# Dense products and attention scores as single float32 products in a two-layer hybrid diffusion trunk step

## The chip, the cores and the metric

The kernel runs on one core of one Trainium2 chip. The metric is the device time of one execution, in microseconds (us). TensorE does the matrix products, VectorE (DVE), ScalarE (ACT) and GpSimd (POOL) the rest, SyncE (SP) issues most loads. All tensors in DRAM are float32.

## What is computed

Two layers over 640 tokens (512 latent, 128 context) of 1024 channels. Each layer has an attention half with four parallel mixers and a feed-forward half with a width-3 convolution; both halves are normed before and after and modulated by a conditioning vector.

```python
def sandwich_layer(x, cvec, mixers, lp):
    mod = jax.nn.silu(cvec) @ lp['w_mod'] + lp['b_mod']
    sh1, sc1, g1, sh2, sc2, g2 = jnp.split(mod, 6, -1)
    h = rmsnorm(x, lp['g_attn_pre']) * (1 + sc1) + sh1
    pa, pb, pc, pd = jnp.split(h @ lp['w_in'], [IN_A, IN_A + IN_B, IN_A + IN_B + IN_C], -1)
    branches, ctx_state = mixers(pa, pb, pc, pd)
    br = jnp.stack(branches, 2)
    gates = jax.nn.sigmoid(h @ lp['w_gate'] + lp['b_gate']).reshape(h.shape[0], h.shape[1], N_BRANCH, D_MODEL)
    merged = jnp.sum(gates * jnp.einsum('blkc,kcd->blkd', br, lp['w_branch']), 2)
    x = x + g1 * rmsnorm(merged @ lp['w_out'], lp['g_attn_post'])
    h = rmsnorm(x, lp['g_ffn_pre']) * (1 + sc2) + sh2
    x = x + g2 * rmsnorm(conv_ffn(h, lp['ffn_w_up'], lp['ffn_conv'], lp['ffn_w_down']), lp['g_ffn_post'])
    return x, ctx_state

def conv_ffn(h, w_up, conv_w, w_down):
    L = h.shape[1]
    u = h @ w_up
    pad = CONV_W // 2
    up = jnp.pad(u, ((0, 0), (pad, CONV_W - 1 - pad), (0, 0)))
    uc = up[:, 0:L] * conv_w[0]
    for j in range(1, CONV_W):
        uc = uc + up[:, j:j + L] * conv_w[j]
    a, gt = jnp.split(uc, 2, -1)
    return (jax.nn.silu(gt) * a) @ w_down
```

The mixers are a 2-D neighbourhood attention (A), a latent attention with low-rank keys (B), a windowed attention with a sink (C) and a pooling mixer (D); A, B and C have four heads each. Latent tokens also read the context keys.

## The kernel before

Operands of the dense products and of the scores are split into two float32r tensors, a high and a low part. `load` brings a weight unit of 128 x 1024 into a `raw` tile (two buffers), and `split` makes the parts: a copy to float32r on ScalarE (L144) and a subtraction on VectorE (L145). The activations that are multiplied with weights are split in the same way when they are written. A dense product is then three products that add up in one PSUM bank:

```python
nc.tensor.matmul(ps, lhsT=hi[:, k, :], rhs=self.hT[:, 0, k, o:o + n], start=k == 0, stop=False)
nc.tensor.matmul(ps, lhsT=hi[:, k, :], rhs=self.hT[:, 1, k, o:o + n], start=False, stop=False)
nc.tensor.matmul(ps, lhsT=lo[:, k, :], rhs=self.hT[:, 0, k, o:o + n], start=False, stop=k == KT - 1)
```

These are lines 536 to 538 (`tposed`: weights stationary, 640 tokens moving in chunks of 384 and 256 columns; the projections of A and D, the gates, and the feed-forward's up projection). Lines 515 to 517 (`nat_step`) have the tokens stationary and 256, 352 or 512 weight columns moving, lines 548 to 550 (`sweep`) the same with 512 for the output and down projections, and lines 1227 to 1229 the branches' products in `gates`. The scores (line 946, `products`) are two such products for A and C and three for B. What multiplies probabilities by values (L938), turns tiles (L155), makes the latent attention's keys, values and queries (L1116, L1122, L1140) and the modulation rows (L370) is plain float32 already.

A layer first runs `attention_phase`. There the order of TensorE's instructions is that in which the code issues them, and `weave` makes it: a chain, such as the attention steps of `pipeline`, yields a time wherever its next product has to wait for other engines, and pieces of a fill (projections or a branch's gates) are issued until the times that they yield in turn add up to it:

```python
for want in chain:
    want -= over
    while want > 0:
        took = next(fill, None)
        if took is None:
            break
        want -= took
    over = max(0, -want)
```

An attention step turns the probabilities of the step before, makes its scores (in two rounds for A and B), and then multiplies the turned probabilities with the values. It asks for the times in `FILL`, 1400 for each pause in the transposes, and a lead at the start. The chain of C is filled with the projections of D and A; those of B's projection, of A and of B with the gates of D, C and A. The gates of B come last, since they need B's output. `out_phase` and `ffn_phase` follow. The feed-forward's 22 hidden tiles go in five groups (`GRP`): `up_pair` makes a group's tiles, `down` projects the group before and adds its part to the sum in `acc`. Layer 1's three modulation banks (`mod_bank`, 8 steps of 4 products each) stand between the hidden tiles of layer 0; those of layer 0 in its attention phase.

Of the kernel before, what the change touches and what calls it, by code (L numbers as in the profile page):

```python
# [12 lines left out]
F32R = mybir.dt.float32r  # L13
# [17 lines left out]
GRP = (4, 4, 4, 4, 6)  # L31
# [16 lines left out]
C_N = C_INV + 2  # L48

# [47 lines left out]
class Kernel:  # L97
# [22 lines left out]
    # ---------------------------------------------------------------- weights  # L120
    def load(self, src, a, b):
        raw = self.t(self.rawp, [128, 1024], "raw", bufs=2)
        rv = raw[:, :a * b].rearrange("p (a b) -> p a b", b=b)
        for j, x in enumerate(src if isinstance(src, list) else [src]):
            p = x.shape[0]
            self.nc.sync.dma_start(out=rv[p * j:p * j + p], in_=x)
        return raw, a, b

    def parts(self, loaded):
        """Loaded weights as two float32r parts."""  # L130
        raw, a, b = loaded
        n = a * b
        w = self.t(self.wp, [128, 2, 1024], "w", F32R)
        self.split(w[:, 0, :n], w[:, 1, :n], raw[:, :n])
        v = w[:, :, :n].rearrange("p s (a b) -> p s a b", b=b)
        return v[:, 0], v[:, 1]

    def unit(self, src, a, b):
        return self.parts(self.load(src, a, b))

    def split(self, hi, lo, src, scale=None):
        nc = self.nc
        if scale is None:
            nc.scalar.copy(hi, src)  # L144
            nc.vector.tensor_tensor(out=lo, in0=src, in1=hi.bitcast(F32), op=ALU.subtract)  # L145
        else:
            nc.scalar.mul(hi, src, scale)
            nc.vector.scalar_tensor_tensor(out=lo, in0=src, scalar=scale, in1=hi.bitcast(F32),
                                           op0=ALU.mult, op1=ALU.subtract)
# [7 lines left out]
    # ---------------------------------------------------------------- set up  # L157
    def run(self):
        nc, tc = self.nc, self.tc
        from contextlib import ExitStack  # L160
        with ExitStack() as es:
            es.enter_context(nc.allow_low_precision("operands split exactly into two float32r parts"))
# [3 lines left out]
            self.wp = es.enter_context(self.pool("w", bufs=5))  # L166
            self.rawp = es.enter_context(self.pool("raw", bufs=2))
# [9 lines left out]
            self.hT = self.t(self.hp, [128, 2, KT, TOK], "hT", F32R)  # L177
# [9 lines left out]
            mod = [self.mod_bank(0, b, hold) for b in (1, 2)]  # L187
            for l in range(self.depth):
                self.attention_phase(l, mod if l == 0 else None, banks if l == 0 else None)
                self.ffn_phase(l)  # L190

    def start(self):
        """Layer 0's first modulation, its normed input and its first projection, by blocks of channels: each
        block's columns of the modulation weights are loaded, its channels modulated, and its products summed."""
# [5 lines left out]
        with self.pool("start", bufs=8) as sp:  # L200
# [5 lines left out]
            for t in range(NT):  # L206
                junk = self.t(self.hp, [128, 2, 1280], "yx", bufs=2)[:, 0, :D]
                self.normed(x[:, t, :], x[:, t, :], junk)
# [41 lines left out]
    def start_products(self, banks, block, unit):  # L250
        hi, lo = unit
        for a in range(block[1]):
            for t in range(NT):
                self.nat_step(banks[t], t, block[0] + a, hi[:, a, :], lo[:, a, :])

    def modulate_block(self, ks, x):
        """Channel tiles ks of all token tiles: transpose, modulate and split into hT."""
        nc = self.nc
        mc = self.lay[0]['mc']
        f = self.t(self.hp, [128, 2, 1280], "yx", bufs=2)[:, 0, :].rearrange("p (k n) -> p k n", k=2)  # L260
        last = self.t(self.psp, [128, 512], "tr", bufs=PSB["tr"])
        for j, kk in enumerate(range(ks.start, ks.stop)):
# [5 lines left out]
            for s, o, n, src in ((0, 0, 512, ps), (1, 512, 128, last[:, 128 * j:128 * j + 128])):  # L268
                a, b = mc[:, 0, 0, s, kk:kk + 1], mc[:, 0, 1, s, kk:kk + 1]
                if j == 0:  # L270
                    nc.scalar.activation(f[:, j, o:o + n], src, AF.Identity, scale=a, bias=b)
                else:
                    nc.vector.tensor_scalar(f[:, j, o:o + n], src, a, b, op0=ALU.mult, op1=ALU.add)
            self.split(self.hT[:, 0, kk, :], self.hT[:, 1, kk, :], f[:, j, :])

    def cond(self):
        nc = self.nc
        raw = self.t(self.rawp, [128, 1024], "raw", bufs=2)[:16]
# [53 lines left out]
    def small(self, l):  # L332
        """The convolution's taps: loads, and a step later their transposes."""
# [20 lines left out]
    # -------------------------------------------------------- modulation rows  # L354
    def mod_bank(self, l, b, hold, late=0):
        """Rows 2b and 2b + 1 of the modulation, by 128 rows of its weights: each load a step ahead of the products."""
        nc, i = self.nc, self.i

        def load(k):
            w = self.t(self.wp, [128, 2048], "w")  # L360
            nc.sync.dma_start(out=w, in_=i['w_mod'][l, 128 * k:128 * k + 128, b * 2048:b * 2048 + 2048])
            return w
# [4 lines left out]
        for k in range(KT):  # L367
            ahead = load(k + 1) if k + 1 < KT else None
            for g in range(4):
                nc.tensor.matmul(ps[32 * g:32 * g + 2, :], lhsT=self.sc[:, k, :], rhs=w[:, 512 * g:512 * g + 512],  # L370
# [23 lines left out]
    def with_steps(self, gen, steps):  # L394
        """gen's pieces with one of steps after each."""
# [5 lines left out]
    def mod_rows(self, l, b, ps, rows):  # L401
        """Modulation rows 2b and 2b+1 of both streams; gates go to DRAM."""
# [1294 lines left out]
```

## Time and profile before

| | |
|---|---|
| median of three runs | 2185.11 us (2182.93 to 2186.3) |
| the profiled execution: its span, which is the time that the profile gives of it | 2180.6 us |
| TensorE busy | 2130.0 us (98% of the span), 13815 products |
| VectorE busy | 1216.8 us (56%) |
| ScalarE busy | 855.7 us (39%) |
| GpSimd busy | 183.3 us (8%) |
| DMA | 221.74 MB, mean 102 GB/s |

The span runs from the first to the last instruction of the program. A product's record is longer than its share of TensorE's time, as products are pipelined; how fast they follow each other is seen from the starts in the timeline. All products are called f32 in the profile, float32r ones too.

### The profile page before, as it was taken

What the parts mean: (1) busy time and instruction counts of PE and PEld (TensorE: products, weight loads), DVE (VectorE), ACT (ScalarE), POOL (GpSimd) and SP (SyncE); (2) the same over time, 40 slices, a digit from 0 to 9 for tenths busy, and PEclk for the clock granted to TensorE, in tenths of its full rate; (3) what the DMA queues carried; (4) which work ended last, traced back from release to release, by engine and by line L of the source; (5) the groups of instructions that cost most, each with busy time, mean ns of one, the idle gap of its engine ahead of it and who ended that gap; (6) DMA issues with size and microseconds to landing.
All of it is one profiled execution on the core that took longest, in us unless ns stands there. A gap on an engine that the chain in (4) does not pass through costs nothing.

```text
span 2180.6 us, 34629 instructions
## 1 busy us (share of the span) xinstructions
PE 2130.0 (98%) x13815; PEld 1928.2 (88%) x13815; DVE 1216.8 (56%) x2207; ACT 855.7 (39%) x1822; POOL 183.3 (8%) x574
## 2 busy tenths in 40 slices
PE   7999999999999999999999999999999999999998
PEld 4779989998889988989878799999998899999996
DVE  3774454653466636456577744556543665556554
ACT  4554344443353333224255543434433533323322
POOL 1102100001021001000021031000000200000001
PEclk9999999999999999999999999999999999999999
DMA  9513221214544444343332132211124322222222
GB/s 303 202 43 101 56 62 46 59 40 156 186 144 150 152 136 156 116 155 89 120 128 81 38 92 64 59 48 52 38 79 154 117 78 78 78 78 78 78 85 94
DMA packets 230476, 221.74 MB, mean 102 GB/s; under 512 B 16084, under 2 KB 196637, under 8 KB 225195
## 3 DMA queue, kind: packets, MB, share of 16 engines
q1 hardware_dynamic: 214000, 191.91, 28.3%
q10 hardware_dynamic: 12026, 21.55, 2.8%
q0 software_dynamic: 4288, 6.07, 1.1%
q8 instruction: 109, 1.79, 0.3%
q14 instruction: 53, 0.43, 0.1%
HBM read 207.94 MB, written 11.56 MB: 101 GB/s over the span
## 4 chain that ended last, share of the span: by engine, by line
PE 89%; DVE 4%; issue 2%; ACT 2%; DMA 1%; POOL 1%; ACTq 0%; DVEq 0%; POOLq 0%
PE mm L536 17%; PE mm L538 16%; PE mm L537 16%; PE mm L548 5%; PE mm L550 5%; PE mm L549 5%; PE tr L155 4%; PE sc L946 3%; PE py L938 2%; PE mm L1227 2%; PE mm L1229 2%; PE mm L1228 2%; PE py L370 1%; PE sc L548 1%; PE sc L549 1%
## 5 line engine op out<-in xcount | busy, mean ns | idle before, releaser
L536 PE MATMUL mm<-hT,w 128*128 128x384 f32 (+1 forms) x2592 | 821.6, 317 | 1.2 <-ACT slab L859 0.9
L538 PE MATMUL mm<-hT,w 128*128 128x384 f32 (+1 forms) x2592 | 801.6, 309 | 1.5 <-DVE w L145 1.5
L537 PE MATMUL mm<-hT,w 128*128 128x384 f32 (+1 forms) x2592 | 800.7, 309 | 0.0
L536 PEld LDWEIGHTS mm<-hT,w 128*128 128x128 f32 x2592 | 491.0, 189 | 33.4 <-issue 17.1
L538 PEld LDWEIGHTS mm<-hT,w 128*128 128x128 f32 x2592 | 491.0, 189 | 3.1 <-DVE w L145 3.1
L537 PEld LDWEIGHTS mm<-hT,w 128*128 128x128 f32 x2592 | 491.4, 190 | 2.0 <-issue 1.4
L145 DVE TENSOR_TENSOR w<-raw,w 128x1024 fp32r<-128x1024 f32 (+2 forms) x263 | 313.4, 1194 | 133.0 <-ACT w L144 131.5
L144 ACT CAST w<-raw 128x1024 fp32r<-128x1024 f32 (+2 forms) x263 | 269.3, 1027 | 205.0 <-PE mm L550 37.3
L1364 DVE TENSOR_SCALAR cv<-ub,taps 128x641 f32<-128x641 f32 x86 | 47.7, 555 | 203.3 <-ACT ub L1358 192.9
L1366 DVE SCALAR_TENSOR_TENSOR cv<-ub,taps,cv 128x641 f32<-128x641 f32 x172 | 152.2, 885 | 5.4
L548 PE MATMUL mm<-w,gT 128*128 128x512 f32 (+1 forms) x352 | 141.4, 402 | 0.0
L549 PE MATMUL mm<-w,gT 128*128 128x512 f32 (+1 forms) x352 | 138.9, 394 | 0.0
L550 PE MATMUL mm<-w,gT 128*128 128x512 f32 (+1 forms) x352 | 138.8, 394 | 0.0
L1209 ACT ACTIVATE th<-mm,cols 128x384 f32<-128x384 f32 (+1 forms) x128 | 67.4, 527 | 148.2 <-PE mm L538 147.9
L1355 ACT COPY ub<-mm 128x384 f32<-128x384 f32 x86 | 41.4, 481 | 164.5 <-PE mm L538 164.4
L1236 DVE SCALAR_TENSOR_TENSOR th<-th,mm 128x384 f32<-128x384 f32 x96 | 45.8, 483 | 100.6 <-PE mm L1229 92.7
L548 PEld LDWEIGHTS mm<-w,gT 128*128 128x128 f32 (+1 forms) x352 | 66.2, 188 | 23.8 <-issue 7.4
L1357 ACT COPY ub<-mm 128x128 f32<-128x128 f32 x86 | 23.0, 267 | 162.4 <-PE mm L538 162.3
L1227 PE MATMUL mm<-yx,w 128*128 128x384 f32 (+1 forms) x256 | 82.8, 323 | 0.0
L1429 DVE TENSOR_TENSOR acc<-acc,mm 128x512 f32<-128x512 f32 x64 | 44.0, 687 | 65.3 <-PE mm L550 64.7
L155 PE MATMUL tr<-cst,P 128*128 128x128 f32 x462 | 67.1, 275 | 13.2 <-DVE P L914 9.2
L550 PEld LDWEIGHTS mm<-w,gT 128*128 128x128 f32 (+1 forms) x352 | 66.0, 188 | 15.7
(305 smaller groups left out, 3152.1 us busy)
## 6 DMA issues: line engine op xcount, KB each, us to landing
w<-in_w_mod_dram SPq DMA_DIRECT2D x46, 1024.0 KB, 4.8
raw<-in_ffn_w_up_dram SPq DMA_DIRECT2D x84, 512.0 KB, 3.9
raw<-in_w_gate_dram SPq DMA_DIRECT2D x64, 512.0 KB, 4.0
raw<-in_ffn_w_down_dram SPq DMA_DIRECT2D x40, 512.0 KB, 3.7
raw<-in_w_in_dram SPq DMA_DIRECT2D x23, 512.0 KB, 4.1
raw<-in_w_out_dram SPq DMA_DIRECT2D x16, 512.0 KB, 6.7
x<-x ACTq DMA_DIRECT2D x14, 512.0 KB, 4.8
raw<-in_w_branch_dram SPq DMA_DIRECT2D x12, 512.0 KB, 3.2
```

What stands on the lines that cost most here:

```text
L144: nc.scalar.copy(hi, src)
L145: nc.vector.tensor_tensor(out=lo, in0=src, in1=hi.bitcast(F32), op=ALU.subtract)
L155: self.nc.tensor.transpose(out, in_, ident)
L536: nc.tensor.matmul(ps, lhsT=hi[:, k, :], rhs=self.hT[:, 0, k, o:o + n], start=k == 0, stop=False)
L537: nc.tensor.matmul(ps, lhsT=hi[:, k, :], rhs=self.hT[:, 1, k, o:o + n], start=False, stop=False)
L538: nc.tensor.matmul(ps, lhsT=lo[:, k, :], rhs=self.hT[:, 0, k, o:o + n], start=False, stop=k == KT - 1)
L548: nc.tensor.matmul(ps, lhsT=lh[:, c], rhs=hi, start=q == 0, stop=False)
L549: nc.tensor.matmul(ps, lhsT=lh[:, c], rhs=lo, start=False, stop=False)
L550: nc.tensor.matmul(ps, lhsT=ll[:, c], rhs=hi, start=False, stop=q == n - 1)
L1209: self.anchor = nc.scalar.activation(th[:, :n], pg[:, :n], AF.Tanh, scale=0.5, bias=L['bh'][:, 8 * br + m:8 * br + m + 1]).ins
L1227: nc.tensor.matmul(pb[:, :n], lhsT=hi[:, 0, ms], rhs=y[:, 0, a, cs], start=a == 0, stop=False)
L1366: nc.vector.scalar_tensor_tensor(out=cv, in0=ub[:, j:j + 641], scalar=tp[:, j:j + 1], in1=cv, op0=ALU.mult, op1=ALU.add)
```

## The change

Weights stay as they are loaded: `unit` loads straight into one of 16 tiles of 128 x 1024 (pool `w`), and `load`, `parts`, `split`, `split_queries`, `split_keys` and the class `Latent` go. Activations are written once, in float32. Each dense product is one float32 product, and so is each product of the scores. The times that pieces of fill yield are worked out anew, from `PER`. The feed-forward keeps all 22 hidden tiles (`gT`, 22 buffers) and has one down projection. Of layer 1's modulation banks the second and third move from the feed-forward of layer 0 into layer 1's attention phase. The factors of one half that went with the splits of `merged` and of the hidden tiles go too; the norm behind each takes `4 * EPS` instead.

```diff
-GRP = (4, 4, 4, 4, 6)
+WBUFS = 16
+PER = 0.842
...
+def took(n):
+
+    return PER * n
...
     def tposed(self, ps, w, c, k0=0, k1=KT):
         o, n = c
         for k in range(k0, k1):
-            nc.tensor.matmul(ps, lhsT=hi[:, k, :], rhs=self.hT[:, 0, k, o:o + n], start=k == 0, stop=False)
-            nc.tensor.matmul(ps, lhsT=hi[:, k, :], rhs=self.hT[:, 1, k, o:o + n], start=False, stop=False)
-            nc.tensor.matmul(ps, lhsT=lo[:, k, :], rhs=self.hT[:, 0, k, o:o + n], start=False, stop=k == KT - 1)
+            self.nc.tensor.matmul(ps, lhsT=w[:, k, :], rhs=self.hT[:, k, o:o + n], start=k == 0, stop=k == KT - 1)
...
         def step(ps, q, o):
-            lh, ll, hi, lo = parts[q]
-            c = slice(o, o + 128)
-            nc.tensor.matmul(ps, lhsT=lh[:, c], rhs=hi, start=q == 0, stop=False)
-            nc.tensor.matmul(ps, lhsT=lh[:, c], rhs=lo, start=False, stop=False)
-            nc.tensor.matmul(ps, lhsT=ll[:, c], rhs=hi, start=False, stop=q == n - 1)
+            lhs, w = parts[q]
+            self.nc.tensor.matmul(ps, lhsT=lhs[:, o:o + 128], rhs=w, start=q == 0, stop=q == n - 1)
...
-    def products(self, outs, parts):
-        """outs[j] = the sum of the products of the pairs in parts[j]."""
-        n = len(parts[0])
-        for q in range(n):
-            for out, p in zip(outs, parts):
-                self.nc.tensor.matmul(out, lhsT=p[q][0], rhs=p[q][1], start=q == 0, stop=q == n - 1)
+    def pair(self, outs, parts):
+
+        for out, (lhs, rhs) in zip(outs, parts):
+            self.nc.tensor.matmul(out, lhsT=lhs, rhs=rhs, start=True, stop=True)
...
             r, ct = self.HALF[j], slice(128 * t, 128 * t + 128)
-            return (x[:, j, a, ct], kk[:, j, c]), (ql[r, a, ct], kk[r, j, c])
+            return x[r, a, ct], kk[r, c]
...
     def between(self, gen, mod):
         for took in gen:
             yield took
             if next(mod, None):
-                yield 850
+                yield 430
...
                     self.tposed(pg[:, :n], u, (o, n), k0, k1)
-                    yield 3 * (k1 - k0) * (n / 2.4 + 2.5)
+                    yield (k1 - k0) * took(n)
...
                 for a in range(2):
-                    hi, lo = wb[a]
-                    nc.tensor.matmul(pb[:, :n], lhsT=hi[:, 0, ms], rhs=y[:, 0, a, cs], start=a == 0, stop=False)
-                    nc.tensor.matmul(pb[:, :n], lhsT=hi[:, 0, ms], rhs=y[:, 1, a, cs], start=False, stop=False)
-                    nc.tensor.matmul(pb[:, :n], lhsT=lo[:, 0, ms], rhs=y[:, 0, a, cs], start=False, stop=a == 1)
-                yield 6 * (n / 2.4 + 2.5)
+                    nc.tensor.matmul(pb[:, :n], lhsT=wb[a][:, 0, ms], rhs=y[:, a, cs], start=a == 0, stop=a == 1)
+                yield 2 * took(n)
...
+            for k in range(2, 22):
+                gts += self.up_pair(l, [k])
+                next(mod, None)
+            self.drain(mod)
+            self.down(l, gts)
```

`FILL`, `PROJ_C_FILL`, `A_LEAD` and the 1400 of the transposes stay. In the changed kernel line 505 is the product of `tposed`, 492 of `nat_step`, 513 of `sweep`, 1155 of the branches, 879 of the scores, 873 of probabilities and values, 140 the transposes.

The change moves instructions on TensorE. The first place is the latent attention of layer 0, in the middle of its steps. Before, a step reads so (`tr` are the banks of the transposes, `P` the probabilities, `sc` the scores, `mm_4803` a gate's bank, `py` the output):

```order
L155 MATMUL tr_4757<-cst_75,P_4677 128x128 x4
L155 MATMUL tr_4763<-cst_75,P_4714 128x128 x4
...
L946 MATMUL sc_4783<-slab_3797,stg_4723 128x320 x2
L946 MATMUL sc_4783<-slab_3797,stg_4724 128x320
...
L536 MATMUL mm_4803<-hT_79,w_4688 128x384
L537 MATMUL mm_4803<-hT_79,w_4688 128x384
L538 MATMUL mm_4803<-hT_79,w_4688 128x384
...
L946 MATMUL sc_4822<-slab_3797,stg_4723 128x320 x2
L946 MATMUL sc_4822<-slab_3797,stg_4724 128x320
...
L938 MATMUL py_4848<-pt_4756,v_3528 64x128 x10
```

And in the changed kernel, from the last gate product before B's own gates on:

```order
L1155 MATMUL mm_3049<-yx_2004,w_2386 128x256
L1155 MATMUL mm_3049<-yx_2004,w_2433 128x256
L879 MATMUL sc_3054<-ka_2453,qa_2452 128x320
L879 MATMUL sc_3055<-ka_2453,qa_2452 128x320
L873 MATMUL py_2985<-pt_3007,v_2454 64x128 x10
L140 MATMUL tr_3083<-cst_72,P_3039 128x128 x4
L140 MATMUL tr_3089<-cst_72,P_3063 128x128 x4
L140 MATMUL tr_3095<-cst_72,P_3039 128x128
L140 MATMUL tr_3095<-cst_72,P_3063 128x128
L879 MATMUL sc_3100<-ka_2453,qa_2452 128x320
L879 MATMUL sc_3101<-ka_2453,qa_2452 128x320
L879 MATMUL sc_3112<-ka_2453,qa_2452 128x320
```

The gate products that stood between a step's scores have gone ahead of it; what follows, up to B's gates, are transposes, scores and products of the attention alone: five whole steps, the second half of another, and two of the context. Layer 1 has the same.

The second place is the end of the window attention. In the changed kernel (`cb` and `acc` hold keys and queries; the last row is the next projection) it reads:

```order
L873 MATMUL py_856<-pt_1011,T_447 64x128 x6
L140 MATMUL tr_1059<-cst_72,P_1034 128x128 x4
L879 MATMUL sc_1068<-cb_446,acc_445 128x384
...
L140 MATMUL tr_1097<-cst_72,P_1070 128x128 x3
...
L879 MATMUL sc_1109<-cb_446,acc_445 128x512
L879 MATMUL sc_1110<-cb_446,acc_445 128x512
...
L140 MATMUL tr_1141<-cst_72,P_1111 128x128 x4
...
L492 MATMUL mm_1270<-w_1275,hT_76 128x352 x2
```

Before, products of lines 536 to 538 stood between those scores and transposes; now the last four steps follow each other without any, in both layers.

## Rows read from the trace of the kernel before

**Rows 1.** The page: busy time of each engine, and the chain by engine.

```profile
PE 2130.0 (98%) x13815; PEld 1928.2 (88%) x13815; DVE 1216.8 (56%) x2207; ACT 855.7 (39%) x1822; POOL 183.3 (8%) x574
...
PE 89%; DVE 4%; issue 2%; ACT 2%; DMA 1%; POOL 1%; ACTq 0%; DVEq 0%; POOLq 0%
```

**Rows 2.** TensorE's largest group by line and form: count | busy us, mean ns.

```profile
L536 PE MATMUL mm<-hT,w 128*128 128x384 f32 x1296 | 444.3, 343 | 0.4 <-ACT hT L144 0.4
```

**Rows 3.** TensorE's timeline, three places: start us, duration us, engine, line, tiles.

```profile
502.70 0.33 PE L536 MATMUL mm<-hT,w 128*128 128x384 f32 x1
...
503.22 0.33 PE L536 MATMUL mm<-hT,w 128*128 128x384 f32 x1
...
505.98 0.28 PE L536 MATMUL mm<-hT,w 128*128 128x256 f32 x1
...
506.34 0.28 PE L536 MATMUL mm<-hT,w 128*128 128x256 f32 x1
...
1121.63 0.39 PE L548 MATMUL mm<-w,gT 128*128 128x512 f32 x1
...
1122.10 0.40 PE L550 MATMUL mm<-w,gT 128*128 128x512 f32 x1
```

**Rows 4.** Line 1116's records, and the timeline around plain float32 products.

```profile
L1116 PE MATMUL sc<-cb x24: 377/378/381, 341.4 to 1427.6; 128*128 128x256 f32 x24
...
344.40 1.03 PE L1116 MATMUL sc<-cb 128*128 128x256 f32 x4
...
345.38 0.28 PE L537 MATMUL mm<-hT,w 128*128 128x256 f32 x1
...
347.92 1.02 PE L1122 MATMUL sc<-cb 128*128 128x512 f32 x2
...
348.95 0.34 PE L1228 MATMUL mm<-yx,w 128*128 128x384 f32 x1
```

**Rows 5.** The timeline of all engines over one step of the latent attention.

```profile
412.76 1.03 PE L155 MATMUL tr<-cst,P 128*128 128x128 f32 x8
...
413.45 0.59 ACT L924 COPY pt<-tr 128x512 f32<-128x512 f32 x1 [0.84 <-PE tr L155]
...
415.36 1.13 PE L946 MATMUL sc<-slab,stg 96*128 96x320 f32 x6
...
417.37 0.53 ACT L1667 ACTIVATE P<-sc,nm 128x320 f32<-128x320 f32 x1 [1.35 <-DVE nm L1663]
...
418.97 1.05 PE L946 MATMUL sc<-slab,stg 96*128 96x320 f32 x6
...
419.95 1.31 PE L938 MATMUL py<-pt,v 128*64 128x128 f32 x20
...
422.65 1.02 DVE L914 TENSOR_SCALAR P<-P,rc 128x640 f32<-128x640 f32 x2
...
423.44 0.82 PE L155 MATMUL tr<-cst,P 128*128 128x128 f32 x6
```

**Rows 6.** The timeline of all engines over one step of the window attention.

```profile
104.08 1.15 PE L946 MATMUL sc<-cb,acc 128*128 128x512 f32 x4
...
105.16 0.38 PE L515 MATMUL mm<-w,hT 128*128 128x256 f32 x1
...
105.26 0.89 DVE L1616 TENSOR_TENSOR sc<-sc,cst 128x128 f32<-128x128 f32 x4 [0.26 <-PE sc L946]
...
109.47 0.88 DVE L914 TENSOR_SCALAR P<-P,rc 128x512 f32<-128x512 f32 x2
```

**Rows 7.** The page: the splits' subtractions, and the third product's group with its wait.

```profile
L538 PE MATMUL mm<-hT,w 128*128 128x384 f32 (+1 forms) x2592 | 801.6, 309 | 1.5 <-DVE w L145 1.5
...
L145 DVE TENSOR_TENSOR w<-raw,w 128x1024 fp32r<-128x1024 f32 (+2 forms) x263 | 313.4, 1194 | 133.0 <-ACT w L144 131.5
```

**Rows 8.** Two stretches: length, busy us of PE, PEld, DVE, ACT, POOL, then clock.

```profile
1708.00:1711.60 3.60, 1.47 (x8) 0.73 (x8) 2.89 (x4) 1.67 (x5) 3.21 (x5) 1.00 0.69 206
1711.60:1715.00 3.40, 3.40 (x15) 3.40 (x14) 3.19 (x7) 3.00 (x7) 0.54 (x1) 0.50 0.57 160
```

More of the change, by code (lines that the diff above doesn't have):

```diff
@@ L118, in ps, with unit @@
         return self.t(self.psp, [128, 512], tag, bufs=PSB[tag])
-    def load(self, src, a, b):
-        raw = self.t(self.rawp, [128, 1024], "raw", bufs=2)
-        rv = raw[:, :a * b].rearrange("p (a b) -> p a b", b=b)
+    def unit(self, src, a, b):
+        w = self.t(self.wp, [128, 1024], "w")
+        wv = w[:, :a * b].rearrange("p (a b) -> p a b", b=b)
         for j, x in enumerate(src if isinstance(src, list) else [src]):
             p = x.shape[0]
[L126 to L149, printed above, removed]
+            self.nc.sync.dma_start(out=wv[p * j:p * j + p], in_=x)
+        return wv
     def row(self, n):
@@ L752, in proj_c @@
         self.transpose(tr[:, :128], ck[:, :128], self.ident)
-        self.split_keys(kk, slice(0, 128), tr[:, :128])
-        nc.gpsimd.tensor_copy(out=kk[:, :, 640:768], in_=kk[:, :, 0:128])
+        nc.scalar.copy(kk[:, 0:128], tr[:, :128])
+        nc.vector.tensor_copy(kk[:, 640:768], tr[:, :128])
         yield PROJ_C_FILL
@@ L1122, in heads_b @@
             nc.tensor.matmul(pk[:, :n], lhsT=wkv[:, 128 * g:128 * g + 128], rhs=ckT[:, o:o + n], start=True, stop=True)
[L1123 to L1124 removed]
+            nc.scalar.copy(kT[0:64, 0, o:o + n], pk[0:64, :n])
+            nc.vector.tensor_copy(kT[0:64, 1, o:o + n], pk[64:128, :n])
             yield 1000
[L1126 to L1127 removed]
+        nc.scalar.copy(kT[64:96, 0], kr)
+        nc.vector.tensor_copy(out=kT[64:96, 1], in_=kr)
         def turn(s, t):
@@ L1268, in out_phase @@
             hs = slice(512 * half, 512 * half + 512)
-            pss = self.sweep(half == 0, [(self.mT[:, 0, k], self.mT[:, 1, k], units[k // 2][0][:, k % 2],
-                                          units[k // 2][1][:, k % 2]) for k in range(KT)],
+            pss = self.sweep(half == 0, [(self.merged[:, k], units[k // 2][:, k % 2]) for k in range(KT)],
                              [128 * t for t in range(NT)])
@@ L1386, in unit_pair @@
     def unit_pair(self, w):
[L1387 to L1398 removed]
+        u = self.t(self.wp, [128, 1024], "w").rearrange("p (a b) -> p a b", b=128)
@@ L1399, in down @@
+        for s in range(2):
+            self.nc.sync.dma_start(out=u[:, :, 64 * s:64 * s + 64], in_=w[:, :, s * D_FF + 2688:s * D_FF + 2752])
+        return u
+    def down(self, l, gts):
+        nc = self.nc
         L = self.lay[l]
-        final = g == len(GRP) - 1
         yb = self.acc[:, :NT * D].rearrange("p (t n) -> p t n", t=NT)
         x_dst = self.o_x if l == self.depth - 1 else L['x2']
-        if final:
-            G = self.gains(l, 1, self.fp, "ub", 643, 4)
-            ss = self.t(self.st, [128, NT, 2], "fss")
+        G = self.gains(l, 1, self.fp, "ub", 643, 4)
+        ss = self.t(self.st, [128, NT, 2], "fss")
+        rows = self.i['ffn_w_down'][l]
@@ L1420, in down @@
-            pss = self.sweep(half == 0, [(gt[:np_, 0], gt[:np_, 1], hi, lo) for gt, np_, hi, lo in units],
-                             [128 * t if t < 4 else 513 for t in range(NT)])
-            if final and half == 1:
+                k = gts[a][0]
+                u = self.down_unit(rows, k, hs)
+                parts += [(gt[:np_], u[:np_, b]) for b, (_, gt, np_) in enumerate(gts[a:a + 2])]
+            pss = self.sweep(half == 0, parts, [128 * t if t < 4 else 513 for t in range(NT)])
+            if half == 1:
@@ L1571, in scores @@
         scs = [K.ps("sc")[:, :n] for _ in range(2)]
-        K.products(scs, [self.qk(g, j, t, slice(k0, k0 + n)) for j in range(2)])
+        K.pair(scs, [self.qk(g, j, t, slice(k0, k0 + n)) for j in range(2)])
         if part == 0:
@@ L1611, in scores @@
         self.P = [K.probs() for _ in range(2)]
-        K.products([scs[j][:, :n] for j in range(2)], [self.qk(a + 2 * j, t, slice(k0, k0 + n)) for j in range(2)])
+        K.pair([scs[j][:, :n] for j in range(2)], [self.qk(a + 2 * j, t, slice(k0, k0 + n)) for j in range(2)])
         for j, sc in enumerate(scs):
```

359 lines of the change are left out of this document (114 added, 245 removed).

## The prediction

> **What bounds the kernel now.** I read the page's busy shares first. TensorE is busy 98% of the span, and the chain that ended last runs through it for 89% [rows 1]; the reader is to see that no other engine comes near, and that whatever TensorE is given more to do lengthens the kernel. The groups by line and form then say what it does: the largest, line 536 with 384 columns, has 1296 records [rows 2], as many as the loops have such products, and lines 537 and 538 have theirs beside it, so a dense product is three records. Its price is read from the distance between starts in the timeline, since the durations (0.28 to 0.40 us) overlap: 0.52 us from a first record to the next product's first one at 384 columns and 0.36 at 256; at 512, 0.47 for two records and so 0.70 for three [rows 3]. By the same slope 352 columns take 0.48.
>
> **What a plain float32 product costs.** The kernel has such products already, in the latent attention's heads. Line 1116 stands 12 times in the program (2 layers, 6 key blocks) and has 24 records: one product is two records. At 256 columns four records and one float32r record behind them pass between 344.40 and 345.38, which is 0.98 us; less 0.12 for the latter, 0.215 a record. At 512 columns, two records and one float32r record of 384 pass in 1.03 us, so 0.43 a record [rows 4]. Both give 0.84 ns per column and record, hence 1.68 ns per column and product: 0.43 us at 256, 0.59 at 352, 0.65 at 384, 0.86 at 512. Nothing excludes a small extra at a change of tile, so I keep 1% (some 20 us) for the range.
>
> **The change, part by part.**
>
> *Dense products.* They stay as many; each exchanges three float32r records for two float32 ones. There are 1424 of 384 columns (2 layers x 8 channel tiles x 81 weight units, and 128 of the branches), 1504 of 256 (the same and 80 values), 680 of 512 (2 layers x 30 units x 5 token tiles x 2 halves, and 80) and 80 of 352. The differences are 0.125, 0.07, 0.16 and 0.11 us: 178 + 105 + 109 + 9 = **401 us more**, all on the engine that sets the end.
>
> *Scores.* Latent: 64 products of 320 columns; three records at about 0.15 (the six of a row pass between 418.97 and 419.95 [rows 5], with a short change of tiles) against 0.54: 6 us more. Neighbourhood and window: a step of two heads took 1.08 us at 512 columns, from 104.08 to 105.16 [rows 6]. After, each head has 64 rows of the array to itself; if both run side by side the pair costs 0.86, if one after the other 1.72. No row has float32 products on halves of the rows. The nearest are those on halves of the columns, probabilities and values: 20 records of 128 columns in 1.31 us [rows 5], where one behind the other they would take 2.15; so I take the lower. Over both layers a pair of heads passes 18,432 columns, 36 times 512: 8 us less, or 23 us more as the upper bound. Scores together: **2 us less**.
>
> *Splits, raw tiles, adds.* 263 subtractions of 1194 ns go, with as many casts; TensorE waited 1.5 us for them in the group of line 538 [rows 7]. Hidden by TensorE's queue, so nothing is gained; were TensorE not the bound, this would be the gain, 313 us of VectorE. The four earlier down projections' adds go the same way. With 16 weight buffers loads start earlier; they are hidden now and stay so. Layer 1's second and third modulation banks move from the first feed-forward phase into its attention: the same 64 products and bytes on SP's queue, ahead by 16 buffers; nothing. The gate rows that GpSimd then makes in layer 1 go through DRAM, as in layer 0 before; they have the first half of the output projection for cover, 40 products or 34 us; without it some 10 us. The inner tiles' last one is needed last by the down projection, at no cost.
>
> *Fill.* This is the term that the diff hides. The attention steps are chains of TensorE, VectorE and ScalarE, and `weave` fills their waits with gate products until their claimed times add up to what the step asks for. The asked times stand unchanged, the claimed ones are now 0.842 ns per column and product, half of the price above and less than the three records claimed. A branch's gates (8 tiles, 10 products each over 640 columns) offer 43 us, where they offered 65; so the fill is used up sooner. The order shows it: from the middle of the latent attention, and in the last steps of the window attention, no product of another kind stands between the steps in either layer, where all were filled before. What a bare step then costs is read from the filled ones:
>
> - Latent [rows 5]: eight transposes from 412.76 on and the first copy, which ends at 414.04 and frees a bank for the last two (0.2 us), then the scores: 1.6 us after the start; scores to the end of the first exponential, when a bank is free, 415.36 to 417.90, 2.5; second head's scores to its transposes, 418.97 to 423.44, 4.5; longer scores 0.3. In sum 8.9 us, in which TensorE has 10 transposes (0.11 each, as the rows of six and of eight differ by 0.21: 1.1), four scores (2.2) and the products of the step before (419.95 to about 421.2): 4.5. So 4.4 us idle. Per layer there are five such steps, three shorter pieces (half a step and two context steps) at some 2.3, and 0.6 at the end: 29.5 us.
> - Window [rows 6]: 105.26 to 109.95 for masks, maximum, exponential and normalization, 4.7 us, with transposes (0.9) and the first scores (0.6) 6.2; TensorE has 2.6 in it. 3.6 us idle, 3.2 at 384 columns; four steps a layer, 14 us.
>
> Both layers: **87 us**. The bounds are nothing (vector work of the removed splits no longer stands before the chain's instructions, and the idle time is partly there today) and 130 (each step half as long again).
>
> *Clock.* TensorE's granted clock fell once before the end: after a stretch of 3.60 us in which it was busy for 1.47, it had half, 1.2 GHz, for the next 3.40 [rows 8]. The bare steps are similar stretches. At half clock, the 2.7 us of a bare step that TensorE has on the chain would double; for some 22 steps that is 0 to 60 us. I take a fifth, **12 us**, as rows 8 show the fall in one place only.
>
> **Sum.** 2180.6 (span) + 401 - 2 + 87 + 12 = 2678.6. The profile gives the execution's span alone; the median of the three runs, 2185.1, lies 4.5 above it, and with as much around it the time is **2683 us**. From no change a measurement of this kernel can tell 0.2%, about 4 us.
>
> **Rivals.**
>
> 1. *The fill does not matter.* The chains run faster without the splits' casts on ScalarE and VectorE, and the waits that exist now (a few tenths each before the transposes) are not repeated. For it: 56% and 39% busy shares [rows 1] fall. Against it: in the filled steps these engines already sat idle between the chain's instructions, so the chain hardly shrinks. It gives 2683 - 87 - 12, about 2585, to 2600 with some of the idle time left.
> 2. *Bare steps at the low clock, and heads one after the other.* For it: rows 8, and that nothing in the trace shows two float32 products on halves of the rows. It gives 2683 + 48 + 31, about 2765. The Trainium skill, in "TensorE: Matmul & The Clock Gate" (the HAM clock gate), says that the engine's clock is halved by default and released by sustained activity; by that rule every bare step is at risk, and the time is the upper one here. The trace agrees at one place, with 0.50 in rows 8.
> 3. *The other side: a float32 product costs one record.* The new planner says so, 0.842 ns per column and product. The point that decides is the count of records per product. If dense ones had one, each would take half, 0.84 ns a column less over the 1.31 million columns of dense products, 1100 us less than in the sum, and the time would be about 1580: faster. Against it stands line 1116, 24 records for 12 products, back to back at 0.215 [rows 4]; a weight tile of 128 by 128 as in the dense ones. The Trainium skill, in "Perfetto Trace Analysis" (Engine Utilization), halves the array's output rate for FP32_LOW_HIGH. Read as the price of a whole product, this is the planner's number and gives the faster time; the trace shows that rate for a record, and two records.
>
> That the change does not do what it says I exclude: the built order has one matmul where there were three, with float32 operands.
>
> **Chances.** Forecast (2635 to 2730): 0.62. Rival 1: 0.14. Rival 2: 0.16. Rival 3: 0.02. The rest, 0.06, is a mixture beyond these. All but the third and a trace of the rest are slower by far more than 0.2%: faster 0.02, within 0.2% 0.01, slower 0.97. Range: from rival 1's upper end, 2595, to rival 2's, 2765; it leaves out some 0.15.
>
> **What would show it.** In the profile after: lines 505 and 513 with 2592 x 2 and 600 x 2 records, starts 0.32 and 0.43 us apart at 384 and 512 columns (a forecast of 0.16 would make rival 3 right); TensorE still over 90% busy, but with idle time of some 100 us more, in two clusters in each layer, each ended by VectorE's normalization or ScalarE's exponentials; VectorE near 40%. A pair of window scores at 512 columns 0.86 us apart confirms the scores' term, 1.7 refutes it. Were the idle time of the clusters below 40 us, my fill term would be wrong; were the granted clock 0.5 over tens of microseconds, the clock term. The prediction as a whole fails if the dense records stand at another distance than 0.84 ns per column.

## The result, and the profile after

The changed kernel takes **2672.63 us** (median of 4 runs, 2671.69 to 2673.98) against 2184.78 us of the kernel before (4 runs): ratio 1.2234, 95% interval 1.2217 to 1.2251. The forecast was 2683. The profiled execution's span is 2669.9 us, 489.3 more than before; the granted clock of TensorE is 0.976 over the span, where it was 0.998.

The page of the changed kernel: busy time, the chain, the largest group by line, and the group of the transposes of the probabilities.

```profile
PE 2583.0 (97%) x10055; PEld 1627.9 (61%) x10055; DVE 772.2 (29%) x1626; ACT 483.1 (18%) x1293; POOL 151.3 (6%) x572
...
PE 95%; DVE 2%; ACT 1%; DMA 1%; issue 0%; ACTq 0%; DVEq 0%; POOLq 0%; POOL 0%
...
L505 PE MATMUL mm<-hT,w 128*128 128x384 f32 (+1 forms) x5184 | 1439.2, 434 | 0.0
...
L140 PE MATMUL tr<-cst,P 128*128 128x128 f32 x462 | 81.5, 320 | 48.0 <-DVE P L849 40.5
```

TensorE still bounds the kernel: it is 97% busy, 98% before [rows 1], and holds 95% of the chain, 89% before, with 10055 records for 13815. Line 505 has 5184 records, two for each of 2592 products, as foretold. The same transposes in the page of the kernel before:

```profile
L155 PE MATMUL tr<-cst,P 128*128 128x128 f32 x462 | 67.1, 275 | 13.2 <-DVE P L914 9.2
```

So their idle time has grown from 13.2 to 48.0 us, 40.5 of them until VectorE's normalization (line 849). VectorE is down to 29%, where I had written "near 40%". That reading was wrong even for the 263 splits of weights alone: without their 313.4 us [rows 7], VectorE's 1216.8 would be some 34% of the new span, and the smaller splits went too. It cost the sum nothing, as that engine bounds nothing.

The price of a record, from TensorE's timeline (start us, duration us, grouped rows; a row's share of the engine's time is the distance to the next start):

```profile
160.63 1.89 PE L505 MATMUL mm<-hT,w 128*128 128x256 f32 x8
162.36 0.82 PE L140 MATMUL tr<-cst,P 128*128 128x128 f32 x6
...
301.93 5.32 PE L505 MATMUL mm<-hT,w 128*128 128x384 f32 x16
307.09 1.04 PE L140 MATMUL tr<-cst,P 128*128 128x128 f32 x8
...
709.92 1.88 PE L513 MATMUL sc<-w,acc 128*128 128x512 f32 x4
711.64 0.59 PE L513 MATMUL mm<-w,acc 128*128 128x512 f32 x1
...
119.27 0.92 PE L879 MATMUL sc<-cb,acc 64*128 64x384 f32 x4
120.12 1.24 PE L505 MATMUL mm<-hT,w 128*128 128x384 f32 x3
```

Eight records of 256 columns pass in 1.73 us, sixteen of 384 in 5.16, four of 512 in 1.72: 0.216, 0.322 and 0.430 us a record, so 0.84 ns per column and record, as in [rows 4] and against the three records of [rows 3]. The last pair of rows is a window score of two heads at 384 columns: four records in 0.85 us. At 0.322 a record, one head after the other would be 1.29, side by side 0.65; so the heads do run side by side, with 0.2 us more, which my 0.86 for the pair at 512 columns had left out. I put it down to the change of tiles at both ends; no run takes it apart. Pairs at 512 columns take 1.06 us at full clock (143.93 to 144.99) and 2.01 at half (182.39 to 184.40, in a bare step), so the 1.7 that I had named as the sign of heads one after the other tells nothing without the clock beside it.

The four clusters of bare steps, as stretches (length, then busy us of PE, PEld, DVE, ACT, POOL, then the granted clock), and for comparison one stretch of filled steps ahead of them:

```profile
165.00:200.00 35.00, 20.97 (x129) 12.77 (x128) 18.22 (x58) 12.90 (x40) 0.00 (x0) 0.78 0.12 32
510.00:546.50 36.50, 36.50 (x180) 26.65 (x180) 15.20 (x38) 9.79 (x29) 1.68 (x4) 1.00 0.17 49
547.00:611.00 64.00, 45.92 (x240) 32.61 (x240) 26.56 (x68) 21.36 (x69) 1.79 (x4) 0.68 0.04 12
1486.00:1519.00 33.00, 19.15 (x106) 11.78 (x108) 18.05 (x56) 10.72 (x32) 0.00 (x0) 0.69 0.14 34
1867.00:1932.00 65.00, 46.30 (x250) 32.59 (x244) 26.77 (x69) 21.71 (x69) 2.43 (x6) 0.68 0.04 15
```

In the filled stretch TensorE is busy throughout at full clock. The clusters, two in each layer, hold 14.0 + 18.1 + 13.9 + 18.7 = 65 us of idle TensorE, and their clock is 0.68 to 0.78. Finer stretches inside the latent cluster, same columns:

```profile
570.40:577.00 6.60, 4.19 (x17) 3.12 (x18) 2.74 (x7) 2.29 (x7) 0.00 (x0) 0.50 0.00 0
577.20:580.50 3.30, 1.76 (x6) 0.62 (x4) 1.47 (x4) 1.13 (x4) 0.00 (x0) 1.00 0.00 0
580.70:587.30 6.60, 5.77 (x33) 4.73 (x32) 2.65 (x7) 2.08 (x6) 0.00 (x0) 0.50 0.00 0
587.50:590.70 3.20, 1.66 (x6) 0.62 (x4) 1.38 (x4) 1.12 (x4) 0.00 (x0) 1.00 0.00 0
```

TensorE alternates, once in each attention step, between half clock (1.2 GHz, 6.6 us or a little more) and full clock (2.4 GHz, some 3.3 us). A step in the timeline of all engines:

```profile
593.26 1.02 DVE L849 TENSOR_SCALAR P<-P,rc 128x640 f32<-128x640 f32 x2
...
593.96 2.51 PE L140 MATMUL tr<-cst,P 128*128 128x128 f32 x10 [0.82 <-DVE P L849]
...
596.26 1.93 PE L879 MATMUL sc<-kb,T 96*128 96x320 f32 x4
...
599.07 0.53 ACT L1515 ACTIVATE P<-sc,nm 128x320 f32<-128x320 f32 x1 [2.19 <-DVE nm L1511]
...
599.74 1.34 PE L879 MATMUL sc<-kb,T 96*128 96x320 f32 x4 [1.54 <-ACT P L1515]
...
601.01 2.39 PE L873 MATMUL py<-pt,v 128*64 128x128 f32 x20
...
603.51 1.02 DVE L849 TENSOR_SCALAR P<-P,rc 128x640 f32<-128x640 f32 x2
...
604.21 0.45 PE L140 MATMUL tr<-cst,P 128*128 128x128 f32 x1 [0.81 <-DVE P L849]
```

From transposes to transposes it takes 10.25 us; I had worked out 8.9. TensorE waits 1.54 us for ScalarE's exponential to free a bank of scores (599.74) and 0.81 for VectorE's normalization (604.21); between these it does its own work slowly: from the transposes to the scores it takes 2.30 us (593.96 to 596.26), where I had worked out 1.6.

### The profile page after: what moved, and what is told of

The parts are those of the page before. It is cut to its first block, busy times and chain, and to the rows that moved or that the text cites. A ratio compares the mean times of both kernels' runs of the same rounds, so it can differ in the third digit from the quotient of the medians.

```text
span 2669.9 us, 25865 instructions
## 1 busy us (share of the span) xinstructions
PE 2583.0 (97%) x10055; PEld 1627.9 (61%) x10055; DVE 772.2 (29%) x1626; ACT 483.1 (18%) x1293; POOL 151.3 (6%) x572
## 3 DMA queue, kind: packets, MB, share of 16 engines
q8 instruction: 80, 1.31, 0.2%
## 4 chain that ended last, share of the span: by engine, by line
PE 95%; DVE 2%; ACT 1%; DMA 1%; issue 0%; ACTq 0%; DVEq 0%; POOLq 0%; POOL 0%
PE mm L505 53%; PE mm L513 16%; PE mm L1155 5%; PE mm L492 4%; PE tr L140 4%; PE sc L513 4%; PE sc L879 4%; PE sc L492 2%; PE py L351 1%; PE py L873 1%; ACT P L1515 1%; PE sc L1072 0%; DVE m L1510 0%; DVE P L849 0%; DVE nm L1486 0%
## 5 line engine op out<-in xcount | busy, mean ns | idle before, releaser
L505 PE MATMUL mm<-hT,w 128*128 128x384 f32 (+1 forms) x5184 | 1439.2, 434 | 0.0
L505 PEld LDWEIGHTS mm<-hT,w 128*128 128x128 f32 x5184 | 974.4, 190 | 421.7 <-issue 25.6
L513 PE MATMUL mm<-w,gT 128*128 128x512 f32 (+1 forms) x704 | 313.5, 595 | 0.0
L1155 PE MATMUL mm<-yx,w 128*128 128x384 f32 (+1 forms) x512 | 152.6, 435 | 0.0
L140 PE MATMUL tr<-cst,P 128*128 128x128 f32 x462 | 81.5, 320 | 48.0 <-DVE P L849 40.5
L1155 PEld LDWEIGHTS mm<-yx,w 128*128 128x128 f32 x512 | 95.8, 190 | 37.7 <-issue 2.0
L1162 DVE SCALAR_TENSOR_TENSOR th<-th,mm 128x384 f32<-128x384 f32 x96 | 46.4, 485 | 236.9 <-PE mm L1155 236.5
L492 PE MATMUL mm<-w,hT 128*128 128x256 f32 (+2 forms) x352 | 113.8, 474 | 0.3 <-ACT hT L251 0.3
L513 PE MATMUL mm<-w,acc 128*128 128x512 f32 x256 | 113.8, 592 | 0.0
L140 PEld LDWEIGHTS tr<-cst,P 128*128 128x128 f32 x462 | 64.2, 164 | 71.2 <-issue 40.2
L492 PEld LDWEIGHTS mm<-w,hT 128*128 128x128 f32 x352 | 67.0, 196 | 36.9 <-issue 22.0
L513 PE MATMUL sc<-w,gT 128*128 128x512 f32 (+1 forms) x176 | 82.7, 592 | 0.0
```

Of the source, the lines that this page charges most:

```text
L140: self.nc.tensor.transpose(out, in_, ident)
L492: self.nc.tensor.matmul(ps, lhsT=self.hT[:, k, 128 * t:128 * t + 128], rhs=w, start=k == 0, stop=k == KT - 1)
L505: self.nc.tensor.matmul(ps, lhsT=w[:, k, :], rhs=self.hT[:, k, o:o + n], start=k == 0, stop=k == KT - 1)
L513: self.nc.tensor.matmul(ps, lhsT=lhs[:, o:o + 128], rhs=w, start=q == 0, stop=q == n - 1)
L1155: nc.tensor.matmul(pb[:, :n], lhsT=wb[a][:, 0, ms], rhs=y[:, a, cs], start=a == 0, stop=a == 1)
L1162: nc.vector.scalar_tensor_tensor(out=th[:, :n], in0=th[:, :n], scalar=1.0, in1=pb[:, :n], op0=ALU.add, op1=ALU.mult)
```

## The experiments

Theory: dense products cost two records each; the attention's waits are no longer filled, since the gates claim half of their price; the clock that falls in the bare steps adds a little. Against it stand the first rival (fill does not matter), the second (the clock takes tens of microseconds, and heads go one after the other), and that the clock costs nothing at all.

**Dense products alone.** The kernel before, one plain product of the high parts for each dense three, in all four places where they stand; here the largest. The low parts are split off as before and left out of the sums.

```diff
-            nc.tensor.matmul(ps, lhsT=hi[:, k, :], rhs=self.hT[:, 0, k, o:o + n], start=k == 0, stop=False)
-            nc.tensor.matmul(ps, lhsT=hi[:, k, :], rhs=self.hT[:, 1, k, o:o + n], start=False, stop=False)
-            nc.tensor.matmul(ps, lhsT=lo[:, k, :], rhs=self.hT[:, 0, k, o:o + n], start=False, stop=k == KT - 1)
+            nc.tensor.matmul(ps, lhsT=hi[:, k, :].bitcast(F32), rhs=self.hT[:, 0, k, o:o + n].bitcast(F32),
+                             start=k == 0, stop=k == KT - 1)
```

> The kernel before, in which every dense product is one plain float32 product of the high parts in place of three float32r ones; the low parts are still made and left out of the sums. Splits, loads, scores, feed-forward blocks and the fill's claimed times stay as before, so the fill lasts as long as before. Theory (price of the records): 404 us more on TensorE, at 0.84 ns per column and record and two records a product, less up to 30 us of short waits that the longer products now cover: 2555 to 2590 us. Rival 1 (the fill does not matter, all of the 488 us are the dense products): 2650 to 2675. Rival 3's price, one record a product, would give about 1500 to 1600.

Measured: 2563.65 us (2563.28 to 2564.27), ratio 1.1737 (1.1717 to 1.1756), inside the expected range. The page's busy times:

```profile
PE 2528.2 (99%) x10127; PEld 1615.0 (63%) x10127; DVE 1228.1 (48%) x2207; ACT 859.4 (34%) x1822; POOL 169.2 (7%) x574
```

TensorE has 3688 records fewer, exactly the 1424 + 1504 + 680 + 80 products of my count, and is busy 398.2 us more than before (2130.0), for 401 worked out. The span (2561.7) grew by 381.1: the other 17.1 us are idle time that went (span less busy: 50.6 before, 33.5 now). So the longer products cover short waits which the sum had left standing; the largest of them, TensorE's idle time before the transposes of the probabilities, fell from 13.2 us to 7.4. Rival 1's price for the dense products and rival 3's are out.

**Fill alone, in the kernel before.** Only what a gate's products claim as fill is changed, to the changed kernel's figures.

```diff
-                    yield 3 * (k1 - k0) * (n / 2.4 + 2.5)
+                    yield (k1 - k0) * 0.842 * n
...
-                yield 6 * (n / 2.4 + 2.5)
+                yield 2 * 0.842 * n
```

> The kernel before, in which only the time that a gate's products claim as fill is changed, to the 0.842 ns per column of the changed kernel; no instruction is added, removed or altered, only their order. Theory (bare attention steps cost idle time and the clock): the latent attention's last steps stand bare, some 30 to 37 us a layer, so 2240 to 2260 us, with the granted clock at 0.5 in stretches of the latent attention. Rival 1 (the fill does not matter): within 10 us of the kernel before, 2175 to 2195.

Measured: 2261.45 us (2257.98 to 2262.12), ratio 1.0349 (1.0334 to 1.0365): 77 us for an order of the same instructions. Its latent attention in the two layers, as stretches:

```profile
462.00:530.00 68.00, 47.73 (x281) 40.03 (x280) 34.49 (x86) 26.01 (x78) 4.15 (x8) 0.66 0.11 32
1585.00:1655.00 70.00, 47.09 (x288) 39.25 (x289) 35.49 (x88) 26.70 (x79) 0.00 (x0) 0.68 0.08 23
```

TensorE sits idle for 20.3 and 22.9 us there, at a clock of 0.66 and 0.68. Rival 1 falls: with float32r products and all splits in place, the same bare steps cost tens of microseconds. The time is 1.5 us over the expected range.

**Claims at the true price, in the changed kernel.** The gates claim twice as much.

```diff
-                    yield (k1 - k0) * took(n)
+                    yield (k1 - k0) * 2 * took(n)
...
-                yield 2 * took(n)
+                yield 4 * took(n)
```

> The changed kernel, in which the time that a gate's products claim as fill is doubled, to the price that its trace shows (two records); no instruction is altered, only their order. Theory: the latent attention is filled again in both layers, where a bare stretch of 64 us holds 27.6 us of products: about 70 us less, 2590 to 2615 us; the window attention's bare steps stay. Rival 1 (the fill does not matter, or the waits only move): 2660 to 2680, the same as the changed kernel. If only the idle time were recovered and the clock stayed low: about 2635.

Measured: 2611.92 us (2610.38 to 2613.14), 60.7 less than the changed kernel and inside the expected range. A stretch of its latent attention, and one of its window attention:

```profile
165.00:201.00 36.00, 21.98 (x132) 13.86 (x131) 19.32 (x62) 12.61 (x39) 0.00 (x0) 0.76 0.12 31
485.00:560.00 75.00, 74.75 (x384) 52.62 (x379) 27.72 (x68) 20.45 (x59) 0.52 (x1) 1.00 0.11 35
```

The latent attention is filled again, busy 74.75 of 75 us at full clock; the window's stretch stays bare (0.76). The gain misses the expected 70 or so, probably since that figure took every filled step to be free of waits: the two latent clusters held 36.8 us of idle time, and the span less the busy time of TensorE fell by 29.1 only (86.9 to 57.8).

**Requests of the window attention halved, and both edits together.** The amounts asked for in the window attention's steps, in the changed kernel; then this and the doubled claims.

```diff
-FILL = ((750, 2550), (1800, 3450), (2400, 2400))
+FILL = ((375, 1275), (1800, 3450), (2400, 2400))
```

> The changed kernel, in which the window attention's steps ask the fill for half of the time (375 and 1275 in place of 750 and 2550); no instruction is altered, only their order. The fill then lasts to the window attention's last steps; the latent attention stays bare. Theory: the window's stretches of 33 to 35 us, with 14 us of idle TensorE in both layers together or a little more and its clock at 0.5 in pieces, shrink: 30 to 44 us less, 2628 to 2643 us. Rival 1 (the waits move elsewhere): 2665 to 2680.

> The changed kernel with both edits: gates' claims doubled, and the window attention's requests halved; no instruction is altered, only their order. Theory: all attention steps are filled, the gains add up (61 us of the doubled claims alone and 30 to 44 of the window's): 2568 to 2582 us, the granted clock 0.99 to 1.0 throughout, and the idle time of TensorE as in the kernel before or below it. What is left over the kernel before is then the dense products' price, about 380 us after their saved waits, as in the run of the dense products alone (2563.7). If the fill only moves waits about: 2600 to 2612.

Measured: 2645.79 us (2643.86 to 2647.6), 26.8 less than the changed kernel, and with both 2587.4 (2587.28 to 2589.58), 85.2 less. The gains add up (60.7 + 26.8 = 87.5). Each of the two lies some microseconds above its range. The likely reason, not tried by itself, is that halved requests spread the same fill thinner, and steps that were full now wait a little. The expectation was also wrong to put 14 us of idle time on both layers together: each layer's window stretch holds 14 by itself (14.0 and 13.9), and the window's gain is about their sum. With both edits the chain's transposes still have this idle time before them:

```profile
L140 PE MATMUL tr<-cst,P 128*128 128x128 f32 x462 | 67.6, 276 | 19.0 <-DVE P L849 16.0
```

**All requests halved.** The three pairs of FILL, and the projection's requests, in the changed kernel.

```diff
-PROJ_C_FILL = 3450
+PROJ_C_FILL = 1725
...
-FILL = ((750, 2550), (1800, 3450), (2400, 2400))
+FILL = ((375, 1275), (900, 1725), (1200, 1200))
```

> The changed kernel, in which every request of the attention's pipelines and of the channel attention's projection is halved, the claims as they stand: nearly the same as claims at the true price everywhere. Theory: as with both edits, 2565 to 2590 us; a little more if the halved requests leave some steps, whose other parts ask as before, with too little fill. If it is the doubled claims of the gates, and not the amount of fill by the clock, that count: about 2630 to 2645.

Measured: 2576.12 us (2575.92 to 2576.4), ratio 1.1796 (1.1778 to 1.1814), 96.5 less than the changed kernel with the same instructions, and inside the expected range. The page's busy times, and the transposes' group:

```profile
PE 2536.6 (99%) x10055; PEld 1593.7 (62%) x10055; DVE 769.3 (30%) x1626; ACT 483.4 (19%) x1293; POOL 152.5 (6%) x572
...
L140 PE MATMUL tr<-cst,P 128*128 128x128 f32 x462 | 66.8, 275 | 13.3 <-DVE P L849 12.1
```

Idle before the transposes is 13.3 us, for 48.0 in the changed kernel and 13.2 in the kernel before; the mean clock is 0.999. Of the 95.7 us between the spans, 49.3 are idle time of TensorE and 46.4 its busy time (2583.0 less 2536.6). It is tempting to book the second part as the clock's price; the next run shows that this is wrong.

**The clock kept up.** The changed kernel, with short products that nobody reads wherever the fill has run out; no work is left out.

```diff
+                    self.busy(int(0.45 * want / 215))
...
+    def busy(self, n):
+        if n:
+            ps = self.ps("mm")
+            for _ in range(n):
+                self.nc.tensor.matmul(ps[:, :128], lhsT=self.ident, rhs=self.cst[:, C_COSB:C_COSB + 128], start=True, stop=True)
```

> The changed kernel, with products of 128 float32 columns that nobody reads (0.215 us each) issued wherever the fill is used up, for 0.45 of the time that the step asked for; all real work unchanged. They keep TensorE busier in the bare steps. Theory with the clock as a cost of its own: the granted clock stays at 1.0 there, and of the about 123 us at half clock some 30 to 50 us come back: 2620 to 2645 us. If the waits alone cost the time and the clock does not: the same as the changed kernel or slower, by up to the 50 us or so of added products: 2670 to 2720.

Measured: 2655.11 us (2654.64 to 2655.47), 17.5 less than the changed kernel: faster, with 532 records more, but between the two ranges. The latent attention's steps in TensorE's timeline, line 600 being the added products:

```profile
586.61 1.09 PE L140 MATMUL tr<-cst,P 128*128 128x128 f32 x8 [0.58 <-DVE P L856]
...
588.24 1.24 PE L886 MATMUL sc<-kb,T 96*128 96x320 f32 x4
589.32 1.28 PE L600 MATMUL mm<-cst 128*128 128x128 f32 x10
591.03 1.34 PE L886 MATMUL sc<-kb,T 96*128 96x320 f32 x4 [0.43 <-ACT P L1522]
592.30 1.31 PE L880 MATMUL py<-pt,v 128*64 128x128 f32 x20
593.54 1.38 PE L600 MATMUL mm<-cst 128*128 128x128 f32 x10
595.50 0.77 PE L140 MATMUL tr<-cst,P 128*128 128x128 f32 x5 [0.57 <-DVE P L856]
```

And the stretch that is bare in the changed kernel:

```profile
547.00:611.00 64.00, 58.27 (x450) 46.23 (x449) 25.33 (x65) 21.65 (x67) 1.97 (x4) 1.00 0.00 1
```

The clock is 1.00, and a step takes 8.89 us (586.61 to 595.50), the 8.9 of the prediction, for 10.25 at the alternating clock; the other three steps of the cluster that run from transposes to transposes take 8.89 to 8.94. So the clock costs 1.36 us in this step, and the other waits are what the step costs at full clock too. The 1.36 lie in two passages: from the transposes to the scores, 2.30 us against 1.63, and from there to the second head's scores, 3.48 against 2.79. The rest of the step takes 4.47 us in both kernels: its scores run at full clock in both, and the products with the values, 2.39 us long at half clock, end before VectorE's normalization does.

Summed over a cluster: the five steps from 548.97 to 604.21, with the context between them, took 55.24 us and take 48.70 (546.80 to 595.50), and the window's three from 173.24 to 196.69 took 23.45 and take 20.45 (174.40 to 194.85; there the clock is still low in part). That is 9.5 us in layer 0 and, taken twice, 19 in all, of which the spans show 16.2; the added products may have cost the rest.

**Scores alone.** The kernel before, with one plain product for each score's two or three; the other parts are left out of the scores.

```diff
-        n = len(parts[0])
-        for q in range(n):
-            for out, p in zip(outs, parts):
-                self.nc.tensor.matmul(out, lhsT=p[q][0], rhs=p[q][1], start=q == 0, stop=q == n - 1)
+        q = 1 if len(parts[0]) == 2 else 0
+        for out, p in zip(outs, parts):
+            self.nc.tensor.matmul(out, lhsT=p[q][0].bitcast(F32), rhs=p[q][1].bitcast(F32), start=True, stop=True)
```

> The kernel before, in which each product of the neighbourhood, window and latent attention's scores is one plain float32 product, on 64 rows for the first two; operands are split as before, and the remaining parts are left out of the scores. Dense products, fill and all else as before. Theory, heads side by side: a pair at 512 columns takes 0.9 to 1.06 us against 1.08 before, latent scores 6 us more in all: 2178 to 2192 us, no change that is large. Rival 2's half, one head after the other: about 31 us more, 2210 to 2220.

Measured: 2192.24 us (2191.86 to 2196.57), ratio 1.0046 (1.0033 to 1.0058), 8 us more, at the upper end of the expected range. Two places of TensorE's timeline, a window pair at 512 columns and a latent pair:

```profile
103.68 1.13 PE L945 MATMUL sc<-cb,acc 64*128 64x512 f32 x4
104.74 0.39 PE L515 MATMUL mm<-w,hT 128*128 128x256 f32 x1
...
418.47 1.24 PE L945 MATMUL sc<-slab,stg 96*128 96x320 f32 x4
419.64 0.33 PE L938 MATMUL py<-pt,v 128*64 128x128 f32 x2
```

The window pair takes 1.06 us, where it took 1.08 [rows 6], so nothing is gained; the latent pair takes 1.17, where it took 0.98 [rows 5], which is 6 us over 32 pairs, as worked out. Heads one after the other (31 us) are excluded.

## Why the prediction was right, step by step

The runs divide the 489.3 us between the spans as follows: dense products alone 381.1, scores alone 9.9, the order of the fill 95.7 (the changed kernel less the one with all requests halved), and 2.6 that no run took apart, if the three add up undisturbed. The remainder is no larger than what the runs of the kernel before differ by (2182.93 to 2186.3).

| term | forecast | measured |
|---|---|---|
| dense products, TensorE's work | +401 | +398.2 |
| short waits that they cover | 0 | -17.1 |
| scores | -2 | +9.9 (8 by the medians) |
| bare steps and their clock | 87 + 12 = 99 | 95.7 |
| everything else in the change | 0 | +2.6 |

*Dense products* were right, count and price, since the kernel before already had products of the new kind and the distance of their starts could be read. The Trainium skill, in "FP8 and Floating Point Precision" (TensorE Precision Notes), has true FP32 make four passes through the array; two records of 0.84 ns per column agree with that as four passes of 0.42, a column a cycle at 2.4 GHz; no row shows the passes themselves.

*Splits, raw tiles, adds at nothing.* Right as far as the runs tell: 2.6 us remain for all of them together, and gains and losses in it may cancel. The step that failed is "TensorE waited 1.5 us for them ... so nothing is gained": I looked for waits on the splits alone, and left all other idle time standing in the sum. 17 us of it went with the longer products; the run that shows it still makes the splits, so it is not their removal.

*Scores.* Right on the mechanism and the latent 6 us; wrong by 8 us on the pairs, where I took the bare time of two heads side by side, 0.86, for a pair that takes 1.06. The remaining 3 to 5 us stay open.

*Fill.* Right: where it would run out, what the waits would end on, and nearly the size. A bare latent step at full clock is 8.9 us, by the prediction and by the run that kept the clock, and that run is still 79.0 us above the one with all requests halved (2655.11 less 2576.12): the fill term at nearly full clock, but for what the added products cost, for 87 forecast. The cluster's idle time, 65 us, is less than the 87 I had worked out, but the term is none the less near its size: I forecast the time by which a step is longer than its work at full clock, and at half clock part of that time is shown as busy. For this reason, and for the 17 us that went elsewhere, the sign "idle time of some 100 us more" failed: TensorE's idle time rose by 36.3 us (50.6 to 86.9).

*Clock.* 12 forecast, 16 to 19 measured, and the nearness is luck: the fifth that I took was a guess. The clock fell in every cluster, for far longer than I assumed: at two levels, a mean of 0.976 means that 2 x 0.024 x 2669.9, some 128 us, were spent at half. My own sign of a wrong clock term ("0.5 over tens of microseconds") came true, and it was a bad sign: how long the clock is low doesn't tell what that costs.

*Rivals.* The first fell by three runs (77 us added by the order of the fill alone, 61 and 96.5 taken back). The second had the fall of the clock right and its price wrong: of 128 us at half, it would lose 60. The Trainium skill, in "TensorE: Matmul & The Clock Gate" (HAM oscillation), describes this pattern, a wait in every round of a loop after which the clock is low each time, and books half of the throttled time as lost, which as an estimate would be 64 us here. The alternation agrees with it, though TensorE was at work for half of the two full-clock stretches shown, after which the clock fell (1.76 of 3.30 and 1.66 of 3.20 us); the price, 16 to 19 us, does not, since only two passages of a bare step grew and the rest went by the time of VectorE and ScalarE. The third fell at line 505's 5184 records.

Two errors of opposite sign, 17 us of waits too many and 12 us too little for the scores, and smaller ones left the sum some 9 us high, well inside the range. That they offset each other is luck too, though the range would have held without it. The lower end of the range is called rival 1's upper end and put at 2595, where that rival goes to 2600; nothing hangs on it. No run with float32 dense products came near the kernel before: with all waits filled, the float32 products alone are 379 us dearer than the three float32r ones.

## What to carry to other kernels

When a kernel fills one engine's waits by claimed times, a change of the claims is a change of the schedule: price the claim against the distance of starts in the trace, and ask where the fill now ends. Here a claim of half the price cost 96 us, a fifth of the whole loss, and halving the requests, two lines of constants, gives it back. Cost a bare step as the longest chain through all engines, not as idle time of one; and after the change, compare steps from start to start, since a lower clock turns idle time into busy time without the step growing as much.

## What the runs showed of the hardware that was not expected

- TensorE's granted clock follows the steps of an attention loop: 0.50 over a stretch of 6.6 us in which it was busy 5.8, then 1.00 over one of 3.2 us in which it was busy 1.7, and so on, one round in each step of 10.25 us. With unread products in the waits it stayed at 1.00 over the latent cluster, and fell only in part of the window's.
- Float32 products of two heads on the two halves of the rows run side by side: four records at 512 columns in 1.06 us, where one behind the other they would take 1.72.
- Half clock cost 1.36 us in a step of 8.89: the passages from the transposes to the scores (2.30 us in place of 1.63) and from these to the next scores (3.48 in place of 2.79) grew, while the products with the values, 2.39 us in place of 1.31, cost nothing.
